# The gates' projection by Strassen's scheme (seven products of halves in place of eight), and the attentions' pools closed at their end

## The chip, the cores and the metric

The kernel runs on one core of one Trainium2 chip. The metric is device microseconds (us) of one execution; three runs of the kernel before stand below. All figures are of the core's five engines: PE (TensorE, matmuls), DVE (VectorE), ACT (ScalarE), POOL (GpSimd) and SP (SyncE, here only the queue that issues loads). PEld is the weight load of PE, which overlaps its matmuls. Each engine carries out its own list of instructions strictly in the order in which it stands; an instruction whose inputs are missing holds up everything behind it on the same engine.

## What is computed

One layer of four parallel mixers on 512 positions of width 1024. Cut to what matters here:

```
h    = rms_norm(x, norm_g)
proj = h @ w_in                       # 1024 -> 11208 columns, split into a_u, ..., d_z and gates
y_a, y_b, y_c, y_d = four mixers (spatial gating, sparse attention, convolution, attention), each * silu(z)
branch_d = einsum('nbsw,nwd->bsnd', ys, w_branch)       # 4 branches, 512 -> 1024
g        = sigmoid(gates.reshape(b, s, 4, 1024))        # gates: the last 4096 columns of proj
merged   = sum_n g_n * branch_d_n
out      = rms_norm(x + merged @ w_out, final_g)
```

The gates are 4096 of the 11208 projected columns, the largest single product of the kernel.

## The kernel before

Every product is in float32r: each operand is split into a high and a low part (`split`: ACT copies to the rounded high part, then another engine subtracts to get the low part), and a product is three matmuls per slice of 128 inputs: high by high, high by low, low by high. The normalized input stands transposed in SBUF as `hh` (high) and `hl` (low), 8 slices of 128 inputs by 512 positions.

`proj_fm` (L114 to L125) makes one tile of 128 projected columns by 512 positions: 24 matmuls, each of 128 weight columns and 512 positions. Its weights come as `raw` (1 MB, 256 columns, two buffers, loaded on SP's queue) and go through `unit` (L109): one split of 128x1024 elements for each 128 columns, by ACT (L80) and, for the low part, by POOL during the attentions and by DVE afterwards (L81, `weights_by`).

After the two attentions (FOX, then DSA) and the convolution come four times a pair of stages, for the branches C, A, D, B in this order:

- `gated` (L718): four tiles of 128 columns of z are projected, passed through a sigmoid (ACT, L726), multiplied by the mixer's output (POOL, L727), by z (DVE, L729), and split into `yh`, `yl`.
- `merge` (L736): eight tiles of 128 gate columns are projected (two to a load of `raw`, so four loads or *pairs*), each passed through a sigmoid (ACT, L771). `product` (L739) multiplies the branch's y by `w_branch` (12 matmuls of 512 positions, `pb`, L744 to L747), DVE multiplies by the gate (L750, L752) and POOL adds to `acc` (L753). A product is issued one projection later than its gate. Weights of the branch come as `rawb`, from the same two buffers as `raw`.

At the end `units_tm` and the `ps_o` products multiply by `w_out`; the last tile's `ps_o` is made in two halves of 256 columns.

A scheduler orders the instructions of each engine within what their data and buffers allow; the loads, splits, matmuls and evictions of one projection then stand beside the matmuls of the one before. There is no order written out by hand around the change. Buffers of SBUF belong to pools: `sb` holds tiles of the tag "qk" and "pt" for the attentions, `wpool` the weights' high and low parts (tags "wh", "wl", four buffers each), `const` small constants and the scores `sc1` to `sc3`.

Of the kernel before, what the change touches and what calls it, by code (L numbers as in the profile page):

```python
# [11 lines left out]
ALU = mybir.AluOpType  # L12
# [21 lines left out]
def hybrid_kernel(ctx: ExitStack, tc, x, norm_g, w_in, gm_ln_g, gm_ln_b, gm_w_s, gm_b_s,  # L34
# [19 lines left out]
    def qk_tile(name, dtype=F32R, shape=(P, 4, 512)):  # L54
        return sb.tile(list(shape), dtype, tag="qk", name=name, bufs=2)

    def pt_tile(name, dtype=F32R, shape=(P, 4, 512)):
        return sb.tile(list(shape), dtype, tag="pt", name=name, bufs=2)

# [46 lines left out]
    def wtiles(shape):  # L106
        return tuple(wpool.tile(shape, F32R, tag="w" + s, name="w" + s, bufs=4) for s in "hl")

# [79 lines left out]
    def load_dv(i):  # L188
# [17 lines left out]
    nc.vector.memset(negh, -0.5)  # L206
    causal = const.tile([P, P], F32, name="causal")
# [3 lines left out]
    up = const.tile([P, S], F32R, name="up")  # L211
    upf = tmp("upf")
# [120 lines left out]
    for u in range(2):  # L333
# [38 lines left out]
        else:  # L372
# [11 lines left out]
            nc.vector.tensor_tensor(cn, rb_, cn, op=ALU.mult)  # L384
            cth = const.tile([P, S], F32R, name="cth")
            ctl = const.tile([P, S], F32R, name="ctl")
            split(cth, ctl, cn, kvg)
# [326 lines left out]

    weights_by["eng"] = nc.vector


    def gated(col, o):  # L718
        y = pair("y")
        for cp in range(2):  # L720
            rz = load_w(col + cp * 256)
            for s in range(2):
                ct = 2 * cp + s
                ps = proj_fm(unit(rz, s))
                sg = tmp("sg")
# [9 lines left out]
    def merge(n, y, first, last):  # L735
        yh, yl = y  # L736
        pend = []

        def product():  # L739
            sg, bh, bl, s, dt = pend.pop()  # L740
            pb = psum("pb")
            cs_ = slice(s * P, (s + 1) * P)
            for k in range(NH):
                nc.tensor.matmul(pb, bh[:, k, cs_], yh[:, k, :], start=(k == 0), stop=False)  # L744
                nc.tensor.matmul(pb, bh[:, k, cs_], yl[:, k, :], start=False, stop=False)  # L745
            for k in range(NH):
                nc.tensor.matmul(pb, bl[:, k, cs_], yh[:, k, :], start=False, stop=(k == NH - 1))  # L747
            acc = accs[dt // 4][:, dt % 4, :]
# [9 lines left out]
        for dq in range(2):  # L758
# [5 lines left out]
            for dp in range(2):  # L764
                rg = load_w(GATES + n * D + (2 * dq + dp) * 256)
                bh, bl = wtiles([P, NH, 256])
                split(bh, bl, rb[:, :, dp * 256:(dp + 1) * 256])
                for s in range(2):
                    ps = proj_fm(unit(rg, s))
                    sg = tmp("sg")  # L770
                    nc.scalar.activation(sg, ps, AF.Sigmoid)  # L771
                    if pend:
                        product()
                    pend.append((sg, bh, bl, s, 4 * dq + 2 * dp + s))
        product()
# [94 lines left out]
```

## Time and profile before

| what | us |
|---|---|
| three runs | 711.07, 710.71, 709.07 |
| their median | 710.71 |
| the profiled execution | 711.89 |
| its span in the trace | 710.2 |
| PE busy | 693.9 (98% of the span) |
| DVE, ACT, POOL busy | 364.5, 275.1, 169.9 |

The profiled execution is 1.18 us longer than the median of the runs and 1.7 us longer than its own span in the trace. The attentions and the convolution end at about 311.7 us of the span; the four pairs of `gated` and `merge` follow until about 660 us, then `w_out`.

The duration of a matmul in the trace includes its passage through the array, and consecutive ones overlap: what one costs in a row of them is the distance between two starts, not its duration. In a timeline each line is one instruction or a run of equal ones (x8): start, duration, engine, line of the kernel, operation, output<-inputs, shape.

### The profile page before, as it was taken

How to read it: one execution, taken by the hardware profiler on the slowest of the kernel's cores; microseconds unless marked ns; L12 is line 12 of the kernel's file. 1: busy time of each engine (PE TensorE's matmuls, PEld its weight loads, DVE VectorE, ACT ScalarE, POOL GpSimd, SP SyncE). 2: the span in 40 equal slices, each digit the busy share in tenths (PEclk: the TensorE clock that was granted, in tenths of full speed). 3: DMA queues.
4: the chain of work that ended last, by engine and by line, in shares of the span. 5: the costliest groups of instructions: out<-in, count | busy, mean ns of one | idle time of the engine just before them, and what ended most of it. 6: DMA issues, size and time to landing. Idle time of an engine off the chain costs nothing.

```text
span 710.2 us, 8000 instructions
## 1 busy us (share of the span) xinstructions
PE 693.9 (98%) x3139; PEld 566.4 (80%) x3139; DVE 364.5 (51%) x638; ACT 275.1 (39%) x439; POOL 169.9 (24%) x110
## 2 busy tenths in 40 slices
PE   7999999988999999999999999999999999999996
PEld 4878767766888888888888888888888888888885
DVE  5825699999953664634233343323522334343454
ACT  4616354354444556433322242223322223333233
POOL 1000487341333323203000021222211132111101
PEclk9999999999999999999999999999999999999999
DMA  6715031312112111242322331322313313133233
GB/s 237 219 64 153 4 118 59 112 59 69 60 60 90 60 60 60 61 147 73 105 83 96 118 114 65 119 77 102 120 60 118 117 61 119 60 118 119 62 117 119
DMA packets 56817, 68.05 MB, mean 96 GB/s; under 512 B 3582, under 2 KB 45067, under 8 KB 56780
## 3 DMA queue, kind: packets, MB, share of 16 engines
q1 hardware_dynamic: 55900, 65.46, 28.3%
q0 software_dynamic: 304, 1.05, 0.4%
q10 hardware_dynamic: 576, 1.05, 0.4%
q8 instruction: 24, 0.39, 0.2%
q14 instruction: 13, 0.11, 0.0%
HBM read 64.80 MB, written 2.10 MB: 94 GB/s over the span
## 4 chain that ended last, share of the span: by engine, by line
PE 85%; DVE 11%; DMA 2%; issue 1%; ACT 0%; SPq 0%; POOLq 0%; POOL 0%; DVEq 0%
PE ps_fm L119 18%; PE ps_fm L120 18%; PE ps_fm L124 18%; PE pb L744 4%; PE pb L745 4%; PE pb L747 4%; DVE sc L474 3%; DVE m L473 2%; PE ps_o L144 2%; PE ps_o L146 2%; PE ps_o L145 2%; DVE sc L466 1%; PE pt_ps L533 1%; PE ps_dv L144 1%; DVE l L511 1%
## 5 line engine op out<-in xcount | busy, mean ns | idle before, releaser
L119 PE MATMUL ps_fm<-hh,wh 128*128 128x512 f32 (+1 forms) x640 | 251.3, 393 | 0.0
L120 PE MATMUL ps_fm<-hl,wh 128*128 128x512 f32 (+1 forms) x640 | 250.0, 391 | 0.0
L124 PE MATMUL ps_fm<-hh,wl 128*128 128x512 f32 (+1 forms) x640 | 162.5, 391 | 0.0
L119 PEld LDWEIGHTS ps_fm<-hh,wh 128*128 128x128 f32 (+1 forms) x640 | 120.1, 188 | 26.0 <-issue 0.9
L120 PEld LDWEIGHTS ps_fm<-hl,wh 128*128 128x128 f32 (+1 forms) x640 | 120.0, 187 | 24.9 <-issue 0.2
L124 PEld LDWEIGHTS ps_fm<-hh,wl 128*128 128x128 f32 (+1 forms) x640 | 119.0, 187 | 25.0 <-issue 0.2
L80 ACT ACTIVATE wh<-raw 128x1024 fp32r<-128x1024 f32 x78 | 82.3, 1056 | 114.1 <-PE ps_fm L120 85.0
L81 DVE TENSOR_TENSOR wl<-raw,wh 128x1024 fp32r<-128x1024 f32 x50 | 61.0, 1222 | 78.4 <-PE ps_fm L124 67.1
L81 POOL TENSOR_TENSOR wl<-raw,wh 128x1024 fp32r<-128x1024 f32 x28 | 69.1, 2474 | 111.9 <-PE ps_fm L124 49.2
L753 POOL TENSOR_TENSOR acc<-acc,sg 128x512 f32<-128x512 f32 x24 | 41.8, 1742 | 155.9 <-DVE sg L752 155.9
L744 PE MATMUL pb<-yh,wh 128*128 128x512 f32 x128 | 49.8, 389 | 0.0
L745 PE MATMUL pb<-yl,wh 128*128 128x512 f32 x128 | 49.8, 389 | 0.0
L81 DVE TENSOR_TENSOR wl<-rawb,wh 128x1024 fp32r<-128x1024 f32 x16 | 19.6, 1225 | 51.3 <-PE ps_fm L124 36.8
L80 ACT ACTIVATE wh<-rawb 128x1024 fp32r<-128x1024 f32 x16 | 16.9, 1057 | 50.6 <-PE ps_fm L120 50.6
L752 DVE TENSOR_TENSOR sg<-pb,sg 128x512 f32<-128x512 f32 x24 | 16.6, 692 | 36.3 <-PE pb L747 36.3
L747 PE MATMUL pb<-yh,wl 128*128 128x512 f32 x128 | 34.2, 389 | 0.0
L519 ACT ACTIVATE l<-l,nm 128x128 f32<-128x128 f32 (+3 forms) x32 | 17.9, 560 | 28.5 <-DVE nm L517 28.5
L771 ACT ACTIVATE sg<-ps_fm 128x512 f32<-128x512 f32 x32 | 19.2, 600 | 24.4 <-PE ps_fm L124 24.4
L747 PEld LDWEIGHTS pb<-yh,wl 128*128 128x128 f32 x128 | 24.0, 188 | 5.0
L744 PEld LDWEIGHTS pb<-yh,wh 128*128 128x128 f32 x128 | 24.0, 188 | 5.0
L745 PEld LDWEIGHTS pb<-yl,wh 128*128 128x128 f32 x128 | 24.0, 188 | 5.0
L145 PE MATMUL ps_o<-wl,mh 128*128 128x512 f32 (+1 forms) x72 | 26.2, 366 | 0.0
(242 smaller groups left out, 913.9 us busy)
## 6 DMA issues: line engine op xcount, KB each, us to landing
raw<-in_w_in_dram SPq DMA_DIRECT2D x39, 1024.0 KB, 4.9
rawb<-in_w_branch_dram SPq DMA_DIRECT2D x8, 1024.0 KB, 4.9
rawt<-in_w_out_dram SPq DMA_DIRECT2D x4, 1024.0 KB, 4.9
xt<-in_x_dram SPq DMA_DIRECT2D x4, 512.0 KB, 8.3
rawt<-in_w_in_dram SPq DMA_DIRECT2D x4, 512.0 KB, 8.4
rawt<-in_w_in_dram SPq DMA_DIRECT2D x2, 1024.0 KB, 5.7
xr<-in_x_dram SPq DMA_DIRECT2D x2, 1024.0 KB, 4.9
out_dram<-o SPq DMA_DIRECT2D x4, 256.0 KB, 2.1
```

Of the source, the lines that this page charges most:

```text
L80: nc.scalar.activation(hi, src, AF.Copy)
L81: eng.tensor_tensor(lo, src, hi.bitcast(F32), op=ALU.subtract)
L119: nc.tensor.matmul(ps[:m], wh[:, k, :], hh[:, k, :], start=(k == 0), stop=False)
L120: nc.tensor.matmul(ps[:m], wh[:, k, :], hl[:, k, :], start=False, stop=False)
L124: nc.tensor.matmul(ps[:m], wl[:, k, :], hh[:, k, :], start=False, stop=(k == NK - 1))
L144: nc.tensor.matmul(ps, ah, wh, start=(k == 0), stop=False)
L145: nc.tensor.matmul(ps, ah, wl, start=False, stop=False)
L474: nc.vector.match_replace(out=scs[i], in_to_replace=m8, in_values=scs[i], imm_value=TAKEN)
L744: nc.tensor.matmul(pb, bh[:, k, cs_], yh[:, k, :], start=(k == 0), stop=False)
L745: nc.tensor.matmul(pb, bh[:, k, cs_], yl[:, k, :], start=False, stop=False)
L747: nc.tensor.matmul(pb, bl[:, k, cs_], yh[:, k, :], start=False, stop=(k == NH - 1))
L753: nc.gpsimd.tensor_tensor(acc, acc, sg, op=ALU.add)
```

## The change

`early` is a pool of its own for what only the attentions and the stages before need (the tags "qk", "pt", "wh", "wl", and `causal`, `up`, `cth`, `ctl`, `sc1` to `sc3`). It is closed after the convolution, and a pool `late` is laid over its place. In it stand weights split by halves (`quarter`: 4 slices of inputs, 128x512 elements, tags "qh", "ql", eight buffers each), the sums `T1` to `T4` and the sums `s1` to `s4`.

A pair of gate tiles (256 columns) is one product of a 2x2 matrix of blocks (two halves of the columns by two halves of the inputs) and a 2x2 matrix of blocks of h (two halves of the inputs by two halves of the positions). Before, that is 8 block products, as 48 matmuls of 512 positions. `gate_pair` forms seven (in Winograd's form): each is 12 matmuls of 256 positions (`half_product`), 84 in all. Their sums are made partly in PSUM (`pa` and `pc` go on accumulating after a partial sum was copied out) and partly by ACT and DVE. Sums of blocks of h (`T1` to `T4`) are made once, after the pool is closed; sums of blocks of the weights (`s1` to `s4`) are made by POOL for each pair. `gated` uses the quarters too (`proj_q`, 24 matmuls of 512 positions as before). A product of the branch is now issued between the block products, of the pair before, so two instead of one are left at the end of a merge. `w_out` is split in eight parts of 128x512 instead of four of 128x1024, and the load of `final_g` waits for the place of `T1`.

```diff
+    early_scope = ExitStack()
+    early = early_scope.enter_context(tc.tile_pool(name="early", bufs=1))
...
     def qk_tile(name, dtype=F32R, shape=(P, 4, 512)):
-        return sb.tile(list(shape), dtype, tag="qk", name=name, bufs=2)
+        return early.tile(list(shape), dtype, tag="qk", name=name, bufs=2)
...
-    weights_by["eng"] = nc.vector
-
+    early_scope.close()
+    late = ctx.enter_context(tc.tile_pool(name="late", bufs=1, reuse_waits="tile"))
+
+    def quarter(src, shape=(P, 4, P)):
+        wh, wl = (late.tile(list(shape), F32R, tag="q" + x, name="q" + x, bufs=8) for x in "hl")
+        split(wh, wl, src)
+        return wh, wl
+
+    def half_product(ps, w, bh, bl, start, stop=True):
+        wh, wl = w
+        for k in range(4):
+            nc.tensor.matmul(ps, wh[:, k, :], bh[:, k, :], start=start and k == 0, stop=False,
+                             skip_group_check=True)
+            nc.tensor.matmul(ps, wh[:, k, :], bl[:, k, :], start=False, stop=False,
+                             skip_group_check=True)
+        for k in range(4):
+            nc.tensor.matmul(ps, wl[:, k, :], bh[:, k, :], start=False, stop=stop and k == 3,
+                             skip_group_check=True)
...
+    T1, T2, T3, T4 = (tsum("t%d" % i) for i in range(1, 5))
+    for kp in range(2):
+        r11, r12, r21, r22 = (sb.tile([P, 2, H], F32, tag="tmp", name="r", bufs=9) for _ in range(4))
+        for r, kh, th in ((r11, 0, 0), (r12, 0, 1), (r22, 1, 1), (r21, 1, 0)):
+            ks, ts_ = slice(4 * kh + 2 * kp, 4 * kh + 2 * kp + 2), slice(th * H, th * H + H)
+            nc.gpsimd.tensor_tensor(r, hh[:, ks, ts_].bitcast(F32), hl[:, ks, ts_].bitcast(F32),
+                                    op=ALU.add)
+        ks = slice(2 * kp, 2 * kp + 2)
+        for (th_, tl_), r, ra, rb_ in ((T1, r11, r12, r11), (T3, r12, r22, r12), (T2, r22, r22, r11),
+                                    (T4, r21, r21, r22)):
+            nc.vector.tensor_tensor(r, ra, rb_, op=ALU.subtract)
+            split(th_[:, ks, :], tl_[:, ks, :], r)
...
+    def gate_pair(raw, between):
+        a11, a12 = raw[:, 0:4, 0:P], raw[:, 4:8, 0:P]
+        a21, a22 = raw[:, 0:4, P:2 * P], raw[:, 4:8, P:2 * P]
+        s1, s2, s3, s4 = (late.tile([P, 4, P], F32, tag="s", name="s", bufs=4) for _ in range(4))
+        nc.gpsimd.tensor_tensor(s1, a21, a22, op=ALU.add)
+        nc.gpsimd.tensor_tensor(s2, s1, a11, op=ALU.subtract)
+        nc.gpsimd.tensor_tensor(s4, a12, s2, op=ALU.subtract)
+        nc.gpsimd.tensor_tensor(s3, a11, a21, op=ALU.subtract)
...
+        pa = bank("pa")
+        half_product(pa, quarter(a11), *fm(0, 0), True)
+        nc.scalar.activation(xu[:, lo], pa, AF.Copy)
+        pc = bank("pc")
+        half_product(pc, quarter(s1), *T1, True)
+        nc.scalar.activation(q, pc, AF.Copy)
+        between(0)
+        half_product(pa, quarter(s2), *T2, False)
+        nc.scalar.activation(xu[:, up_], pa, AF.Copy)
+        pb_ = bank("pb_")
+        half_product(pb_, quarter(a12), *fm(1, 0), True)
+        nc.vector.tensor_tensor(g1[:, lo], pb_, xu[:, lo], op=ALU.add)
+        half_product(pc, quarter(s4), *fm(1, 1), False)
+        nc.vector.tensor_tensor(g1[:, up_], pc, xu[:, up_], op=ALU.add)
+        nc.scalar.activation(g1, g1, AF.Sigmoid)
+        half_product(pa, quarter(s3), *T3, False)
+        nc.vector.tensor_tensor(g2[:, up_], pa, q, op=ALU.add)
+        nc.scalar.activation(g2[:, up_], g2[:, up_], AF.Sigmoid)
+        between(1)
+        half_product(pa, quarter(a22), *T4, False)
+        nc.scalar.activation(g2[:, lo], pa, AF.Sigmoid)
+        return g1, g2
...
-                rg = load_w(GATES + n * D + (2 * dq + dp) * 256)
-                bh, bl = wtiles([P, NH, 256])
-                split(bh, bl, rb[:, :, dp * 256:(dp + 1) * 256])
+                gs = gate_pair(load_w(GATES + n * D + (2 * dq + dp) * 256), product)
                 for s in range(2):
-                    ps = proj_fm(unit(rg, s))
...
+                    c0 = dp * 256 + s * P
+                    pend.append((gs[s], quarter(rb[:, :, c0:c0 + P]), 4 * dq + 2 * dp + s))
+        product()
         product()
```

Up to the end of the convolution all engines keep the order that they had, but for the splits of the weights of the first `gated`, which leave the convolution's rows, and the load of `final_g`. Two places after it show what moves.

The list of ACT at the end of the attentions, before; `pth` are the attention's transposed probabilities, `od` its output, `wh<-raw` and `wh<-rawb` weights' high parts (the first two of them for the last convolution tile and for a tile of z):

```order
L80 ACTIVATE pth<-pt_ps 128x3x128
L80 ACTIVATE wh<-raw 128x1024
L80 ACTIVATE pth<-pt_ps 128x4x128
L80 ACTIVATE wh<-raw 128x1024
L545 ACTIVATE od<-po 128x512
L80 ACTIVATE wh<-raw 128x1024
L80 ACTIVATE wh<-rawb 128x1024
L726 ACT_TABLE_LOAD
```

The same place now, with the buffers' numbers; `t1` to `t4` are the high parts of the sums of h, `qh` the quarters of the first z weights:

```order
L83 ACTIVATE pth_2647<-pt_ps_2731 128x4x128
L548 ACTIVATE od_1982<-po_2755 128x512
L83 ACTIVATE t1_2818<-r_2822 128x512
L83 ACTIVATE t3_2820<-r_2823 128x512
L83 ACTIVATE t2_2819<-r_2825 128x512
L83 ACTIVATE t4_2821<-r_2824 128x512
L83 ACTIVATE t1_2818<-r_2842 128x512
L83 ACTIVATE t3_2820<-r_2843 128x512
L83 ACTIVATE t2_2819<-r_2845 128x512
L83 ACTIVATE t4_2821<-r_2844 128x512
L83 ACTIVATE qh_2866<-raw_2864 128x512
```

The weights of z no longer stand among the attention's last rows: the first of them stands behind all eight splits of the sums of h.

The list of POOL from the convolution's last step (`cv`) through the first `gated` into the first `merge`, before:

```order
L696 TENSOR_SCALAR cv<-cc,prm 128x512 x2
L801 DMA fgB<-in_final_g_dram 128x1024
L727 TENSOR_TENSOR sg<-sg,oc 128x512 x4
L727 TENSOR_TENSOR sg<-sg,oa 128x512 x4
L753 TENSOR_TENSOR acc<-acc,sg 128x512 x8
```

The same place now; `r` are sums of the high and low parts of blocks of h, `s` the sums of blocks of the gates' weights:

```order
L699 TENSOR_SCALAR cv<-cc,prm 128x512 x2
L762 TENSOR_TENSOR r<-hh,hl 128x512 x8
L822 TENSOR_TENSOR sg<-sg,oc 128x512
L779 TENSOR_TENSOR s<-raw 128x512
L780 TENSOR_TENSOR s<-s,raw 128x512
L822 TENSOR_TENSOR sg<-sg,oc 128x512
L781 TENSOR_TENSOR s<-raw,s 128x512
L782 TENSOR_TENSOR s<-raw 128x512
L822 TENSOR_TENSOR sg<-sg,oc 128x512 x2
L779 TENSOR_TENSOR s<-raw 128x512
```

POOL's list had four multiplications in the first `gated` and none in the first `merge`; eight sums of h now stand ahead of the first multiplication, and the four sums of each pair's weights stand between and behind them.

## Rows read from the trace of the kernel before

**Rows 1.** The page: busy time, share and count of PE; its granted clock, forty slices.

```profile
PE 693.9 (98%) x3139; PEld 566.4 (80%) x3139; DVE 364.5 (51%) x638; ACT 275.1 (39%) x439; POOL 169.9 (24%) x110
PEclk9999999999999999999999999999999999999999
```

**Rows 2.** Windows: stretch, its length, busy time of each engine, clock, DMA share, GB/s.

```profile
344.00:667.00 323.00, 323.00 (x1427) 267.54 (x1426) 116.10 (x123) 98.55 (x122) 62.34 (x36) 1.00 0.30 98
```

**Rows 3.** Timeline of PE in a merge: starts of two products and two projections.

```profile
480.37 0.39 PE L744 MATMUL pb<-yh,wh 128*128 128x512 f32 x1
...
483.09 0.39 PE L744 MATMUL pb<-yh,wh 128*128 128x512 f32 x1
...
485.81 0.39 PE L119 MATMUL ps_fm<-hh,wh 128*128 128x512 f32 x1
...
491.25 0.39 PE L119 MATMUL ps_fm<-hh,wh 128*128 128x512 f32 x1
```

**Rows 4.** Timeline of PE: first and last of the 48 matmuls of 256 columns.

```profile
698.01 0.28 PE L144 MATMUL ps_o<-wh,mh 128*128 128x256 f32 x1
...
703.64 0.28 PE L146 MATMUL ps_o<-wh,ml 128*128 128x256 f32 x1
```

**Rows 5.** Groups by form: count, busy us, mean ns of one, idle before and its releasers.

```profile
L80 ACT ACTIVATE wh<-raw 128x1024 fp32r<-128x1024 f32 x78 | 82.3, 1056 | 114.1 <-PE ps_fm L120 85.0 <-PE pb L745 25.0 <-PE ps_va L146 2.6
L81 DVE TENSOR_TENSOR wl<-raw,wh 128x1024 fp32r<-128x1024 f32 x50 | 61.0, 1222 | 78.4 <-PE ps_fm L124 67.1 <-ACT wh L80 11.3
L771 ACT ACTIVATE sg<-ps_fm 128x512 f32<-128x512 f32 x32 | 19.2, 600 | 24.4 <-PE ps_fm L124 24.4
L81 DVE TENSOR_TENSOR yl<-y,yh 128x512 fp32r<-128x512 f32 x16 | 11.1, 693 | 11.2 <-ACT yh L80 11.2
L80 ACT ACTIVATE yh<-y 128x512 fp32r<-128x512 f32 x16 | 10.1, 632 | 40.6 <-DVE y L729 40.6
```

**Rows 6.** Timeline of PE: end of the convolution's last projection, start of z's first.

```profile
309.92 1.98 PE L124 MATMUL ps_fm<-hh,wl 128*128 128x512 f32 x8
311.73 0.39 PE L119 MATMUL ps_fm<-hh,wh 128*128 128x512 f32 x1
```

**Rows 7.** Timeline of POOL from the convolution's last step to the first z.

```profile
299.46 1.60 POOL L696 TENSOR_SCALAR cv<-cc,prm 128x512 f32<-128x512 f32 x1 [6.36 <-DVE cc L693]
307.49 0.60 POOL L801 DMA_DIRECT2D fgB<-in_final_g_dram  x1 [6.43 <-PE po L90]
318.63 1.28 POOL L727 TENSOR_TENSOR sg<-sg,oc 128x512 f32<-128x512 f32 x1 [10.54 <-ACT sg L726]
```

**Rows 8.** Timeline of DVE over the same stretch.

```profile
298.67 0.69 DVE L693 TENSOR_TENSOR cc<-ps_fm,cc 128x512 f32<-128x512 f32 x1 [2.15 <-PE ps_fm L124]
299.28 1.21 DVE L81 TENSOR_TENSOR wl<-raw,wh 128x1024 fp32r<-128x1024 f32 x1
300.41 0.68 DVE L81 TENSOR_TENSOR ptl<-pt_ps,pth 128x512 fp32r<-128x512 f32 x1
301.09 1.54 DVE L699 SCALAR_TENSOR_TENSOR cv<-cc,prm,cv 128x511 f32<-128x511 f32 x2
```

**Rows 9.** DVE (first two) and POOL (next two) timelines at 97 to 112 us; POOL's additions (min/median/max).

```profile
99.07 1.60 DVE L466 SCALAR_TENSOR_TENSOR sc<-relu,prm,sc 128x384 f32<-128x384 f32 x1
110.41 1.70 DVE L81 TENSOR_TENSOR val<-vn,vah 128x512 fp32r<-128x512 f32 x1
97.56 2.69 POOL L81 TENSOR_TENSOR wl<-raw,wh 128x1024 fp32r<-128x1024 f32 x1
109.82 1.75 POOL L610 TENSOR_TENSOR vn<-vn,gmp 128x512 f32<-128x512 f32 x1
L753 POOL TENSOR_TENSOR acc<-acc,sg x24: 1283/1714/2205, 435.1 to 661.0; 128x512 f32<-128x512 f32 x24
```

**Rows 10.** The page: loads of weights, count, KB each, us from issue to landing.

```profile
raw<-in_w_in_dram SPq DMA_DIRECT2D x39, 1024.0 KB, 4.9
```

**Rows 11.** Windows of 1 us in and behind PE's longest gap (columns as in rows 2).

```profile
168.00:169.00 1.00, 0.31 (x1) 0.30 (x2) 1.00 (x3) 1.00 (x4) 1.00 (x1) 1.00 0.00 0
170.00:171.00 1.00, 1.00 (x6) 1.00 (x6) 1.00 (x4) 0.39 (x3) 0.07 (x1) 0.50 0.02 8
173.00:174.00 1.00, 1.00 (x6) 0.82 (x5) 1.00 (x4) 0.31 (x1) 0.00 (x0) 1.00 1.07 377
```

More of the change, by code (lines that the diff above doesn't have):

```diff
@@ L54, in qk_tile @@
     def qk_tile(name, dtype=F32R, shape=(P, 4, 512)):
[L55 removed]
+        return early.tile(list(shape), dtype, tag="qk", name=name, bufs=2)
     def pt_tile(name, dtype=F32R, shape=(P, 4, 512)):
[L58 removed]
+        return early.tile(list(shape), dtype, tag="pt", name=name, bufs=2)
     def pair(name):
@@ L106, in wtiles @@
     def wtiles(shape):
-        return tuple(wpool.tile(shape, F32R, tag="w" + s, name="w" + s, bufs=4) for s in "hl")
+        return tuple(early.tile(shape, F32R, tag="w" + s, name="w" + s, bufs=4) for s in "hl")
     def unit(raw, s):
@@ L206, in hybrid_kernel @@
     nc.vector.memset(negh, -0.5)
-    causal = const.tile([P, P], F32, name="causal")
+    causal = early.tile([P, P], F32, name="causal")
     nc.gpsimd.memset(causal, 0.0)
@@ L210, in hybrid_kernel @@
                             pattern=[[-1, P]], channel_multiplier=1)
-    up = const.tile([P, S], F32R, name="up")
+    up = early.tile([P, S], F32R, name="up")
     upf = tmp("upf")
@@ L384, in hybrid_kernel @@
             nc.vector.tensor_tensor(cn, rb_, cn, op=ALU.mult)
-            cth = const.tile([P, S], F32R, name="cth")
-            ctl = const.tile([P, S], F32R, name="ctl")
+            cth = early.tile([P, S], F32R, name="cth")
+            ctl = early.tile([P, S], F32R, name="ctl")
             split(cth, ctl, cn, kvg)
@@ L450, in scores_topk @@
             n = (i + 1) * P
-            sc = const.tile([P, n], F32, name="sc%d" % i)
+            sc = early.tile([P, n], F32, name="sc%d" % i)
             scs[i] = sc
@@ new lines, in proj_q, with tsum @@
+    def proj_q(raw, s):
+        cs_ = slice(s * P, (s + 1) * P)
+        w = [quarter(raw[:, 4 * i:4 * i + 4, cs_]) for i in range(2)]
+        ps = mm.tile([P, S], F32, tag="mm", name="ps_z")
+        for i in range(2):
+            half_product(ps, w[i], hh[:, 4 * i:4 * i + 4, :], hl[:, 4 * i:4 * i + 4, :], i == 0, i == 1)
+        return ps
+    H = S // 2
+    def tsum(name):
+        t = late.tile([P, 2, 4, H], F32R, tag="ts", name=name, bufs=4)
+        return t[:, 0], t[:, 1]
+    T1, T2, T3, T4 = (tsum("t%d" % i) for i in range(1, 5))
@@ new lines, in fm, with bank @@
+    def fm(k, t):
+        return hh[:, 4 * k:4 * k + 4, t * H:t * H + H], hl[:, 4 * k:4 * k + 4, t * H:t * H + H]
+    def gate_pair(raw, between):
[6 more added lines that the diff above has]
+        nc.gpsimd.tensor_tensor(s3, a11, a21, op=ALU.subtract)
+        g1, g2 = tmp("g1"), tmp("g2")
+        xu, q = tmp("xu"), tmp("q", cols=H)
+        lo, up_ = slice(0, H), slice(H, S)
+        def bank(name):
+            return mm.tile([P, S], F32, tag="mm", name=name)[:, lo]
+        pa = bank("pa")
[20 more added lines that the diff above has]
+        return g1, g2
@@ L723, in gated @@
                 ct = 2 * cp + s
-                ps = proj_fm(unit(rz, s))
+                ps = proj_q(rz, s)
                 sg = tmp("sg")
@@ L737, in merge, with product @@
         pend = []
-        def product():
-            sg, bh, bl, s, dt = pend.pop()
+        def product(_=None):
+            if not pend:
+                return
+            sg, (bh, bl), dt = pend.pop(0)
             pb = psum("pb")
-            cs_ = slice(s * P, (s + 1) * P)
             for k in range(NH):
-                nc.tensor.matmul(pb, bh[:, k, cs_], yh[:, k, :], start=(k == 0), stop=False)
-                nc.tensor.matmul(pb, bh[:, k, cs_], yl[:, k, :], start=False, stop=False)
+                nc.tensor.matmul(pb, bh[:, k, :], yh[:, k, :], start=(k == 0), stop=False)
+                nc.tensor.matmul(pb, bh[:, k, :], yl[:, k, :], start=False, stop=False)
             for k in range(NH):
-                nc.tensor.matmul(pb, bl[:, k, cs_], yh[:, k, :], start=False, stop=(k == NH - 1))
+                nc.tensor.matmul(pb, bl[:, k, :], yh[:, k, :], start=False, stop=(k == NH - 1))
             acc = accs[dt // 4][:, dt % 4, :]
@@ L788, in hybrid_kernel @@
         cs_ = slice(half * 512, (half + 1) * 512)
-        us = units_tm(w_out[0], cs_)
+        us = []
+        for kh in range(2):
+            raw = load_tm(w_out[0], kh, cs_)
+            us += [quarter(raw[:, j, :], (P, 512)) for j in range(4)]
         xr = raw_tile([P, NT, 512], "xr")
@@ L793, in contrib @@
         def contrib(ps, t, k, c):
-            wh, wl = us[k // 2]
+            wh, wl = us[k]
             mh, ml = mrg[k // 4]
             ts_ = slice(t * P, (t + 1) * P)
-            term_tm(ps[:, c], mh[:, k % 4, ts_], ml[:, k % 4, ts_], wh[:, k % 2, c], wl[:, k % 2, c], k)
+            term_tm(ps[:, c], mh[:, k % 4, ts_], ml[:, k % 4, ts_], wh[:, c], wl[:, c], k)
         if half == 0:
-            fgB = pt_tile("fgB", F32, (P, D))
+            fgB = late.tile([P, D], F32, tag="ts", name="fgB", bufs=4)
             nc.gpsimd.dma_start(fgB, bcast_rows(final_g, D))
```

5 lines of the change are left out of this document (removed).

## The prediction, made before the changed kernel ran

> **What bounds the kernel now.** I read the page's shares of busy time first. PE is busy 693.9 of 710.2 us, its granted clock stands at full in nearly every slice [rows 1], DVE comes to about half of that. The average could hide a stage, so the second view is the windows: from 344 to 667 us, which holds the merges, PE is busy 323.00 of 323.00 us at clock 1.00, while DVE needs 116, ACT 99 and POOL 62 [rows 2]. Nothing but less work for PE can shorten this stretch, and every microsecond that PE waits there, now or after the change, is added whole. The third view is the timeline of PE: the rate of a row of matmuls is the distance of starts. A projection's 24 matmuls of 512 positions run from 485.81 to 491.25, 0.2267 us each; a product's 12 take 2.72 [rows 3].
>
> **What the change takes off PE.** Per pair of gate tiles 48 matmuls of 512 positions become 84 of 256. The only long row of 256 columns stands at the tail: from the first to the last of 48 starts 5.63 us, over 47 distances 0.1198 each [rows 4]. Half of 0.2267 is 0.1133, so each half matmul carries 0.0064 us of its own. There are 4 merges of 4 pairs: 16 x 48 x 0.2267 = 174.1 us go, 16 x 84 x 0.1198 = 161.0 come, which is **-13.1**. By the count of columns alone it would be 174.1/8 = 21.8; the small extra takes 8.7 of it. The Trainium skill ("TensorE: Matmul & The Clock Gate", "Back-to-back issue gap") gives about 131 ns for a sustained matmul of 512 columns and 81 ns at 128; two of 256, an estimate between these, would then cost more than one of 512, and the change would be slower by tens of us. Both rows speak against that here, so it enters no term.
>
> **What it adds on other engines.** Per pair POOL makes four sums of 128x512 elements, in addition to two accumulations; one such operation takes 1.28 us alone [rows 7] and 1.28 to 2.2 in a merge [rows 9]. Why up to 2.2: DVE operations with two inputs in SBUF and POOL operations don't run side by side here. A DVE operation that begins at 99.07 ends at 100.67, just behind the end of POOL's split at 97.56 + 2.69 = 100.25; a second ends at 112.11, behind POOL's end at 109.82 + 1.75 = 111.57 [rows 9]. A waiting engine gets in at the other's end. The Trainium skill ("SBUF — State Buffer", "Who interferes with whom") says that such a pair shares one read port, taken by whichever issues first for its whole length; it speaks against this change, which puts sums on both engines at once. The two rows agree with it; by it the transition below costs 8.8, without it 2.8.
>
> Per pair this shared path then carries 6 x 1.28 = 7.7 us of POOL and nine DVE splits of half size (seven quarters of the gate, two of the branch). A DVE split of 1024 takes 1.22, one of 512 positions 0.69 [rows 5]; half of the former is 0.61, I take 0.65: 9 x 0.65 = 5.9. Together 13.6, against PE's 84 x 0.1198 + 24 x 0.2267 = 15.5 per pair. It fits, narrowly; a chain in it need not.
>
> **The transition.** Before, z's first weights are split on ACT and DVE well ahead; z's first projection follows the convolution's last one at 311.73 without a gap [rows 6]. Now eight sums on POOL, eight subtractions on DVE and eight splits of the T sums stand ahead of the first quarter of z, on both engines. No row shows them. The walk:
> - POOL is free for them after the last `cv`: 299.46 + 1.60 = 301.06 [rows 7], and DVE still has two steps of 1.54 together for the last `cv` [rows 8].
> - If the two engines exclude each other, one path holds 8 x 1.28 + 1.54 + 8 x 0.65 = 17.0 us, to 318.0. Then DVE has one output of the convolution, eight low halves of T and the first low quarter of z: 0.61 + 8 x 0.61 + 0.69 = 6.2, to **324.2**. (0.61 is also the distance of two starts on DVE, 298.67 to 299.28 [rows 8].)
> - ACT has T's last high half and the first high quarter at 0.63 each [rows 5], to 319.3. PE can run 16 matmuls with high quarters before it needs the first low one. Undisturbed that one would be due at 311.73 + 16 x 0.2267 = 315.4. Loss 324.2 - 315.4 = 8.8.
> - PE then has stood for about 7 us. After a gap of PE in the kernel before the granted clock was 0.50 from 170 to 171 and back at 1.00 by 173 [rows 11], so 2.4 GHz falls to 1.2 and returns in some 3 us. The 16 matmuls cover most of that while ql is awaited; 16 x 0.2267 = 3.6 is the most it can add, I take none.
>
> Bounds: without exclusion POOL ends at 301.06 + 10.24 = 311.3, DVE's last subtraction at 312.0, the low quarter at 318.2: loss 2.8. With exclusion and a slow clock 12.4. I take **+8.8**, as rows 9 show the exclusion twice.
>
> **The first merge.** The first load of gate weights for a later pair waits for a buffer that z's last quarters release. In the kernel before a load of 1 MB lands 4.9 us after its issue [rows 10]. With the low quarters 0.61 apart, z's last is cut at about 324.2 + 7 x 0.61 = 328.5 and that load lands at 333.4; the last z projection ends at 311.73 + 4 x 5.44 + 8.8 = 342.3. That is 9 us ahead, but the sums of the weights share POOL with the four multiplications of z, and ACT's copy `q` of the first partial sum stands behind a split that waits for the next load. Walking the queues through the first pair gives waits of PE of 1.4 us at the bank of the third block product, freed late by a DVE multiplication, and 2.3 at the one with `s4`: **+3.7**, from 1 (exclusion absent) to 6.
>
> **The later merges.** There the loads come earlier. The same walk leaves slack of about 0.5 us at two places per merge: `q` behind the split of the next load, and the copies of `pa` behind the sum `s2`. I take 0.3 for each merge, three of them: **+1.0**, from 0 to 8.
>
> **Edits at nothing.** The splits of `w_out` have half the size and twice the number on engines far from full [rows 2]; the last two products of a merge, where one stood, are followed by PE's own work. Fewer ACT evictions (0.60 each, 32 of them [rows 5]) are replaced by seven half-size ones per pair, on an engine busy 99 of 323 us. The load of `final_g`, POOL 0.60 [rows 7], moves behind the use of `T1`, and is needed only in the tail. If one of these shows, it is below 1 us each.
>
> **Sum.** 711.89 - 13.1 + 8.8 + 3.7 + 1.0 = 712.3 for the profiled execution, which is 1.18 above the median of the runs, so **711.1** as a median.
>
> **Rivals.**
> 1. *The gain arrives.* POOL and DVE do run side by side on these shapes, or the waiting engine gets in more cheaply: transition 2.8, first merge 2, later ones 0.5. 711.89 - 13.1 + 5.3 - 1.18 = **702.9**. For it: that POOL is busy only 62 of 323 us [rows 2], so that most of its work can find room. Against it: rows 9, and that the eight sums stand in one row with the eight subtractions.
> 2. *The pairs are bound by the chain, slower.* One buffer of raw weights serves all four pairs of a merge in turn while the other holds the branch's weights; next load (4.9 us [rows 10]), sums `s1`, `s2`, `s4` (3 x 1.28 at least, up to 3 x 2.2 [rows 9]), split, matmul is a chain within each pair of 15.5 us. If each of POOL's sums is stretched to the 1.71 that is the median of the accumulations [rows 9], six of them take 10.3 rather than 7.7; the 2.6 more eat the 0.5 of slack and PE loses 2.1 in each of the 12 later pairs at worst, or about 0.6 if the loads ahead absorb most. At 0.6 a pair: 711.1 + 12 x 0.6 - 1.0 = **717.3**. It decides from 0.2 us per pair on, which is slower by over 0.3%. For it: the narrow 13.6 against 15.5; against it: median 1.71 is with splits of double size, whose halves block less long.
> 3. *The matmuls of 256 don't keep 0.1198* with other halves of `hh` as the moving side: at 0.130 the 1344 matmuls give back 13.7 us and the change gains nothing: 711.1 + 13.7 = 724.8. Only the tail row [rows 4] speaks to it, and against it.
>
> **How the numbers follow.** Forecast (PE gains 13, waits take all of it back, to within 0.3%, which is about what a measurement of this kernel can tell from no change: 708.6 to 712.8): 0.35, its own range 707 to 714 before it passes into the rivals. Rival 1: 0.33. Rival 2: 0.28, rival 3: 0.04. Faster 0.33, same 0.35, slower 0.32. The range reaches from 702.5, which leaves a third of rival 1 out, to 719, which leaves out rival 3 and a fifth of rival 2: some 0.2 in all.
>
> **What would show it.** Right: a gap of PE of about 7 us behind the convolution's last projection, ended by ACT's first quarter, and then a wait for DVE's `ql`; POOL's eight sums and DVE's subtractions alternating from 301 to 318; starts of the half products 0.12 apart; waits of PE in the first merge at `pb_` and at the product with `s4`; later merges with PE busy throughout. Wrong: subtractions running beside POOL's sums, PE gaps in every pair, or starts 0.13 apart.

## The result: slower by 2.8%

| | before | after |
|---|---|---|
| median of the runs, us | 710.89 | 730.88 |
| lowest and highest | 709.07, 711.99 | 729.57, 731.95 |
| span of the profiled execution | 710.2 | 728.8 |
| z's first projection starts / `w_out` starts | 311.7 / 659.9 | 314.9 / 678.5 |

The ratio is 1.0283 (95% interval 1.0259 to 1.0307). The forecast was 711.1 with a range up to 719.0: the change is slower by 20 us, outside the range.

The page of the changed kernel first (columns as in [rows 1]):

```profile
PE 693.9 (95%) x3715; PEld 591.0 (81%) x3715; DVE 493.4 (68%) x822; ACT 330.4 (45%) x631; POOL 276.6 (38%) x182
PEclk9999999989999999999999999999999899999998
```

PE has 576 matmuls more, of half the size, and exactly the busy time that it had: what the change saves there was lost again, mostly on slower matmuls (table below). The span is longer by 18.6 us, all of it idle time. The window that answers to [rows 2], a little longer since the stage is:

```profile
344.00:678.00 334.00, 320.08 (x1979) 289.54 (x1978) 224.26 (x278) 149.64 (x294) 151.72 (x97) 0.97 0.30 99
```

Before, PE was busy for all of the stretch at clock 1.00; now 14 us are missing and the clock is 0.97. POOL went from 62 to 152 us, DVE from 116 to 224.

To see how the loss divides I took the starts of PE's rows from its timeline and compared their distances with 0.2267 us for 512 positions and 0.1198 for 256 [rows 3, 4]. The column on the clock holds the matmuls that started while the granted clock was 0.50; the last one holds mostly waits of 0.1 to 0.2 us and the part of each long wait that the end of the matmul ahead of it covers.

| stretch (us) | over those distances | idle, in waits over 0.3 | matmuls at clock 0.50 | the rest |
|---|---|---|---|---|
| 308.2 to 338.3, end of convolution and z | 6.6 | 4.7 | 1.6 | 0.3 |
| 338.3 to 411.1, first merge | 10.7 | 5.9 | 3.1 | 1.7 |
| 411.1 to 499.5, second z and merge | 4.7 | 3.4 | 0.0 | 1.3 |
| 499.5 to 590.6, third | 7.3 | 3.3 | 2.8 | 1.2 |
| 590.6 to 678.5, fourth | 4.2 | 2.2 | 1.6 | 0.4 |
| sum | 33.5 | 19.5 | 9.1 | 4.9 |

Less the 13.1 that the smaller products save this is 20.4. The spans differ by 18.6, since PE also ended the convolution some 1.7 us earlier in this execution; that point lies between 308 and 312.5 us in the runs.

The same wait stands in merges one to three, 2.73 or 2.74 us each: PE stands in front of the third pair's last block product, with the fourth pair begun. This is PE's timeline there in the first merge (start, duration, engine, line, operation; in brackets the idle time and what ended it):

```profile
387.45 0.40 PE L840 MATMUL pb<-yh,qh 128*128 128x512 f32 x1
390.57 0.58 PE L732 MATMUL pa<-t,qh 128*128 128x256 f32 x1 [2.73 <-DVE g L806]
390.95 0.41 PE L734 MATMUL pa<-t,qh 128*128 128x256 f32 x1
391.17 0.41 PE L732 MATMUL pa<-t,qh 128*128 128x256 f32 x1
```

PE has the last block product of the third pair before it, which goes on accumulating in `pa`; DVE must first have read `pa` into `g2` (L806). Behind the wait the starts lie 0.21 to 0.22 apart, not 0.12. DVE's timeline over the same stretch:

```profile
383.89 1.23 DVE L84 TENSOR_TENSOR ql<-raw,qh 128x512 fp32r<-128x512 f32 x1 [5.00 <-ACT qh L83]
385.04 0.41 DVE L803 TENSOR_TENSOR g<-pc,xu 128x256 f32<-128x256 f32 x1
385.37 1.44 DVE L84 TENSOR_TENSOR ql<-s,qh 128x512 fp32r<-128x512 f32 x1
386.74 0.68 DVE L846 TENSOR_TENSOR acc<-pb,g 128x512 f32<-128x512 f32 x1
387.34 1.18 DVE L84 TENSOR_TENSOR ql<-s,qh 128x512 fp32r<-128x512 f32 x1
388.44 1.75 DVE L84 TENSOR_TENSOR ql<-raw,qh 128x512 fp32r<-128x512 f32 x1
390.11 0.41 DVE L806 TENSOR_TENSOR g<-pa,q 128x256 f32<-128x256 f32 x1
```

And POOL's:

```profile
383.27 1.29 POOL L779 TENSOR_TENSOR s<-raw 128x512 f32<-128x512 f32 x1 [8.88 <-DMA raw<-in_w_in_dram]
384.65 1.62 POOL L780 TENSOR_TENSOR s<-s,raw 128x512 f32<-128x512 f32 x1
386.35 1.61 POOL L781 TENSOR_TENSOR s<-raw,s 128x512 f32<-128x512 f32 x1
387.93 1.71 POOL L782 TENSOR_TENSOR s<-raw 128x512 f32<-128x512 f32 x1
```

Read together: the load of the fourth pair lands at about 383.2, POOL and DVE have both stood idle for it, and both start within 0.7 us. The four sums run in a row; the four splits of the new pair beside them take 1.18 to 1.75 us where 0.65 was assumed, two-input operations whose ends follow POOL's ends (385.12 behind 384.56, 386.81 behind 386.27, 388.52 behind 387.96, 390.19 behind 389.64). The operation for which PE waits, 0.41 us long, is the seventh in that row. The operations with one input in PSUM (L803, L846) keep their 0.41 and 0.68.

In the fourth merge PE waits for the load itself: ACT splits it as soon as it has landed, and PE starts behind ACT (first ACT, then PE).

```profile
652.57 0.63 ACT L83 ACTIVATE qh<-raw 128x512 fp32r<-128x512 f32 x1 [4.64 <-DMA raw<-in_w_in_dram]
653.25 0.49 PE L732 MATMUL pa<-hh,qh 128*128 128x256 f32 x1 [2.17 <-ACT qh L83]
```

Merges two and three have the same kind of wait, 0.66 and 0.54 us, some 6.7 us ahead of the long one. Of the 8.8 us of waits in merges two to four, 3.4 are thus for the load and 5.5 for DVE's addition.

What follows the wait in the first merge is seen in windows of PE (columns as in [rows 2]):

```profile
388.00:390.00 2.00, 0.00 (x0) 0.00 (x0) 2.00 (x2) 0.63 (x1) 1.64 (x1) 1.00 0.00 0
390.00:392.00 2.00, 1.43 (x6) 1.43 (x7) 1.60 (x4) 1.45 (x4) 0.00 (x0) 0.64 0.00 0
392.00:394.00 2.00, 2.00 (x10) 1.90 (x9) 1.30 (x3) 1.56 (x4) 0.00 (x0) 0.51 0.00 0
394.00:396.00 2.00, 2.00 (x11) 1.68 (x11) 0.43 (x2) 0.63 (x1) 0.00 (x0) 1.00 0.93 292
```

PE was idle for 2.7 us; then the granted clock falls to 0.5, from 2.4 to 1.2 GHz, for some three us although PE is busy throughout, and returns. Such stretches make the clock's column of the table, 9.1 us in all. Not every wait has one. In the second merge the wait for DVE is as long and the clock stays at full speed:

```profile
480.53 0.39 PE L732 MATMUL pa<-t,qh 128*128 128x256 f32 x1 [2.73 <-DVE g L806]
```

```profile
479.00:481.00 2.00, 0.47 (x4) 0.47 (x5) 2.00 (x3) 0.49 (x2) 2.00 (x2) 1.00 0.00 0
481.00:483.00 2.00, 2.00 (x15) 1.83 (x14) 2.00 (x3) 2.00 (x6) 0.28 (x1) 1.00 0.00 0
483.00:485.00 2.00, 2.00 (x14) 1.80 (x13) 1.39 (x4) 0.94 (x3) 0.00 (x0) 1.00 0.38 97
```

Of the five waits of over 2 us in the merges four had a stretch at 0.50, of 3.4 us each and in the third merge of 6.8.

### The profile page after: what moved, and what is told of

The parts are those of the page before. It is cut to its first block, busy times and chain, and to the rows that moved or that the text cites. A ratio compares the mean times of both kernels' runs of the same rounds, so it can differ in the third digit from the quotient of the medians.

```text
span 728.8 us, 9819 instructions
## 1 busy us (share of the span) xinstructions
PE 693.9 (95%) x3715; PEld 591.0 (81%) x3715; DVE 493.4 (68%) x822; ACT 330.4 (45%) x631; POOL 276.6 (38%) x182
## 4 chain that ended last, share of the span: by engine, by line
PE 50%; DVE 24%; DMA 12%; issue 7%; POOL 4%; ACT 3%; SPq 0%; POOLq 0%; DVEq 0%; ACTq 0%
DMA raw<-in_w_in_dram 10%; DVE ql L84 8%; PE ps_fm L122 5%; PE ps_fm L127 5%; PE ps_fm L123 5%; DVE sc L477 3%; DVE m L476 3%; PE pb L843 2%; PE pb L841 2%; ACT qh L83 2%; PE pb L840 2%; PE pa L732 2%; PE ps_o L147 2%; PE ps_o L148 2%; PE ps_o L149 2%
## 5 line engine op out<-in xcount | busy, mean ns | idle before, releaser
L84 DVE TENSOR_TENSOR ql<-raw,qh 128x512 fp32r<-128x512 f32 x80 | 75.5, 951 | 80.0 <-ACT qh L83 65.0
L122 PE MATMUL ps_fm<-hh,wh 128*128 128x512 f32 (+1 forms) x256 | 102.9, 403 | 0.0
L123 PE MATMUL ps_fm<-hl,wh 128*128 128x512 f32 (+1 forms) x256 | 101.8, 398 | 0.0
L84 DVE TENSOR_TENSOR ql<-s,qh 128x512 fp32r<-128x512 f32 x64 | 73.4, 1161 | 4.3 <-ACT qh L83 3.9
L127 PE MATMUL ps_fm<-hh,wl 128*128 128x512 f32 (+1 forms) x256 | 68.0, 396 | 0.0
L779 POOL TENSOR_TENSOR s<-raw 128x512 f32<-128x512 f32 x16 | 20.6, 1289 | 106.6 <-DMA raw<-in_w_in_dram 106.6
L732 PE MATMUL pa<-t,qh 128*128 128x256 f32 x192 | 50.5, 293 | 8.2 <-DVE g L806 8.2
L122 PEld LDWEIGHTS ps_fm<-hh,wh 128*128 128x128 f32 (+1 forms) x256 | 48.6, 190 | 11.3 <-issue 1.2
L123 PEld LDWEIGHTS ps_fm<-hl,wh 128*128 128x128 f32 (+1 forms) x256 | 48.5, 190 | 10.2 <-issue 0.2
L127 PEld LDWEIGHTS ps_fm<-hh,wl 128*128 128x128 f32 (+1 forms) x256 | 47.1, 187 | 10.1 <-issue 0.2
L734 PE MATMUL pa<-t,qh 128*128 128x256 f32 x192 | 50.1, 291 | 0.0
L732 PEld LDWEIGHTS pa<-t,qh 128*128 128x128 f32 x192 | 38.2, 199 | 10.3 <-DVE g L806 9.1
L734 PEld LDWEIGHTS pa<-t,qh 128*128 128x128 f32 x192 | 38.4, 200 | 0.8
```

Of the source, the lines that this page charges most:

```text
L84: eng.tensor_tensor(lo, src, hi.bitcast(F32), op=ALU.subtract)
L122: nc.tensor.matmul(ps[:m], wh[:, k, :], hh[:, k, :], start=(k == 0), stop=False)
L123: nc.tensor.matmul(ps[:m], wh[:, k, :], hl[:, k, :], start=False, stop=False)
L127: nc.tensor.matmul(ps[:m], wl[:, k, :], hh[:, k, :], start=False, stop=(k == NK - 1))
L732: nc.tensor.matmul(ps, wh[:, k, :], bh[:, k, :], start=start and k == 0, stop=False, skip_group_check=True)
L734: nc.tensor.matmul(ps, wh[:, k, :], bl[:, k, :], start=False, stop=False, skip_group_check=True)
```

## The experiments

Two questions stood at the start: whether the waits of the merges come from the path that POOL and DVE share or from loads that land too late; and what the setup of `T1` to `T4` costs. All times are medians; ratios are to the kernel before, run on the same chip (710 to 711 us), with 95% intervals. Diffs are against the changed kernel.

**e1: POOL's sums only write.** The line of `s1`; `s2`, `s4` and `s3` likewise.

```diff
-        nc.gpsimd.tensor_tensor(s1, a21, a22, op=ALU.add)
+        nc.gpsimd.memset(s1, 0.01)
...
```

> POOL's four sums of each pair's gate weights are replaced by four POOL operations of the same size that only write (the sums are then a constant, so the gates are not the reference's); all else stays. Theory A (the shared path): the changed kernel loses 26 us in its merges because DVE's low splits of the weights run 1.2 to 1.8 us instead of 0.65 while POOL's sums read. Without those reads the splits take 0.65 to 0.7 and the waits of PE for DVE g of 2.7 us vanish: 708 to 714 us. Theory B (late loads): the gate weights land too late, since all four pairs of a merge use one buffer in turn; DVE's and POOL's work hardly matters, the waits stay near 2 us each: 726 to 731.

Measured: 706.26, ratio 0.9946 (0.9923 to 0.9969). The second, third and fourth stages of z and merge took 84.0 us each; their matmuls alone are 96 x 0.2267 + 336 x 0.1198 + 96 x 0.2267 = 83.8. As Theory A expected, but the edit took away two things, the reads and the chain from the load to the sums.

**e2: a buffer of its own for the branch's weights.** To make room, the fourth sum `s3` is also made later, behind the copy `q`, and the sums have three buffers instead of four.

```diff
-            rb = raw_tile([P, NH, 512], "rawb")
...
+                rb = late.tile([P, NH, 256], F32, tag="rb", name="rawb", bufs=1)
+                rg = load_w(GATES + n * D + cb)
+                nc.sync.dma_start(rb, w_branch[0, n, :, cb:cb + 256].rearrange("(k p) c -> p k c", p=P))
```

> The branch's weights get a buffer of their own (loads of 512 KB, 256 columns), so both 1 MB buffers serve the gates in turn; the fourth sum is made a little later to make room. Theory A: DVE's splits still take 1.2 to 1.8 us beside POOL's sums, and the order of the engines is much the same; some waits get shorter, 724 to 730 us. Theory B: the loads land 5 us and more ahead, the waits of PE in the later merges go, 710 to 716.

Measured: 706.78, ratio 0.9945 (0.9925 to 0.9964), better than either theory expected, again with stages of 84.0 us each. Groups by form over the second to fourth stage (count, busy us, mean ns, idle time before), the changed kernel first:

```profile
L84 DVE TENSOR_TENSOR ql<-raw,qh 128x512 fp32r<-128x512 f32 x53 | 52.3, 986 | 57.6 <-ACT qh L83 51.6 <-issue 4.9 <-PE pb__5354 L734 1.1
L84 DVE TENSOR_TENSOR ql<-s,qh 128x512 fp32r<-128x512 f32 x48 | 57.2, 1207 | 2.9 <-ACT qh L83 2.5
L779 POOL TENSOR_TENSOR s<-raw 128x512 f32<-128x512 f32 x12 | 15.5, 1290 | 79.1 <-DMA raw<-in_w_in_dram 79.1
```

and e2:

```profile
L84 DVE TENSOR_TENSOR ql<-raw,qh 128x512 fp32r<-128x512 f32 x54 | 52.8, 977 | 12.2 <-ACT qh L83 8.5 <-PE ps_z L737 3.4
L84 DVE TENSOR_TENSOR ql<-s,qh 128x512 fp32r<-128x512 f32 x48 | 41.3, 861 | 22.1 <-PE ps_z L737 9.6 <-ACT qh L83 7.4 <-PE pa L737 4.6
L779 POOL TENSOR_TENSOR s<-raw 128x512 f32<-128x512 f32 x11 | 15.2, 1385 | 11.7 <-issue 3.9 <-DMA raw<-in_w_in_dram 3.7 <-DVE ql L84 3.4
```

POOL waited 79 us for loads in the changed kernel and 3.7 here; DVE's splits are still long, 0.86 to 0.98 us in the mean (0.99 to 1.21 before), and PE waits for none of them in these stages. So neither theory holds alone. The edit also broke up POOL's row: the four sums of a pair no longer follow each other (they start at 448.5, 453.2, 455.0 and 461.8 us for one pair of the second stage), so this run takes away two things, too.

**e3: the sums of h behind the first z.** The block that makes `T1` to `T4` is written behind `yc = gated(C_Z, oc)`.

> The sums T1 to T4 of h are written behind the first stage of z instead of ahead of it. Both theories: the gap of 4.7 us before z's first projection and the slow clock behind it (1.7 us) go; if the sums then delay the first pair by as much, the time stays. Theory 'the setup costs 4.8 us' expects 725 to 727; a rival, that the sums only move their price into the first merge, 730 to 733.

Measured: 737.93, ratio 1.0391 (1.0371 to 1.0411): worse than both. The gap ahead of z is gone, but from z's start to the end of the first merge it takes 106.6 us against 96.2, with waits of up to 4.0 us for the splits of the sums, then between PE's single matmuls. The price only moved, and grew.

**e4: the pools and quarters alone.** `gate_pair` makes two plain projections; no sums.

> The pools are closed and the weights split by quarters as in the change, but the gates are projected by eight products (24 matmuls of 512 positions per tile) and no sums are made. If closing the pools and the quarters cost nothing by themselves, 709 to 713 us; if the moved splits ahead of z cost, 714 to 718.

Measured: 710.82, ratio 1.0003 (0.9987 to 1.0020). Closing the pools and splitting by quarters cost nothing; PE has no wait from 300 to 670 us.

**e5: as much POOL time, hardly a read.** Two `memset` of the sum, then one column of it formed from the operands.

> Two things fell in e1 at once: POOL no longer reads beside DVE, and its operations no longer wait for the load and for each other. Here each of the four sums is two operations that only write (0.53 us each in e1) and one that reads one column in 128 of the same operands, so POOL waits for the load and for its own chain as in the changed kernel, about 1.2 us a link, but hardly reads (the gates are not the reference's). Theory A (the shared path is what makes the chain too long): DVE's low splits take 0.65 to 0.75 us, the waits in the merges go, 705 to 712 us. Rival (POOL's chain from the load to the sums is itself too long, whatever DVE does): the waits of 2.7 us for DVE g stay, 722 to 731.

Measured: 705.94, ratio 0.9921 (0.9897 to 0.9944). Inconclusive: the writes depend on nothing, POOL's list had them ahead of the load, and behind it stood four operations of 0.21. The chain had fallen with the reads, as in e1.

**e6: the sums on DVE.** `nc.gpsimd` becomes `nc.vector` in the four lines.

> The four sums of each pair stand on DVE instead of POOL, one word in each of four lines; the loads keep their two buffers. Theory A: no POOL operation reads beside a split but the additions into acc, DVE does 4 x 0.69 = 2.8 us more a pair and comes to some 11 of 15.5; most waits go, 706 to 714 us. Rival (DVE becomes the bound, the sums queue in it behind the splits of the pair before): 718 to 730.

Measured: 709.46, ratio 0.9977 (0.9957 to 0.9998). The later stages take 84.0 to 84.1. In the first merge the wait of 2.2 for ACT's `q` stays.

**e7: e2, and two tiles of z ahead of the sums of h.** In `gated`; `mid` is the block that makes `T1` to `T4`.

```diff
+            pz = [proj_q(rz, s) for s in range(2)]
+            if mid is not None and cp == 0:
+                mid()
...
```

> e2's buffer for the branch's weights, and the first two tiles of z are projected ahead of the sums T of h, the other two behind; the high quarters of the first two stand on ACT ahead of T's splits. Of the 706.8 of e2 the gap of 4.85 us ahead of z and the 1.7 of the slow clock go, a wait of about 1.2 for the first low quarter comes: 700 to 703. If the sums then come late for the first pair as in e3: 706 to 714.

Measured: 703.48, ratio 0.9893 (0.9862 to 0.9924), just above the 700 to 703. The gap of 4.7 became a wait of 2.95 for `ql`, which DVE still gives only behind its eight subtractions, and 2.9 us lost on slow matmuls behind it, at clock 0.50 from 316 to 323 us (the 0.96 in the next run's expectation is too small); the first merge has no wait left.

**e8: e7, with the sums of the high and low parts of h on DVE too.**

> e7, and the eight sums of the high and low parts of h (the first step of T1 to T4) stand on DVE instead of POOL. In e7 PE still waited 2.95 us for the first low quarter and ran 0.96 longer at the slow clock, since DVE's eight subtractions alternated with POOL's sums, 15.2 us for both. Sixteen operations of 0.65 to 0.69 on DVE alone take 11, of which five stand ahead of the last step of the attention. If the shared path is what holds ql back, both losses go: 699 to 701 us. Rival (DVE's sums delay the attention's last product by as much as they save): 702 to 706.

Measured: 700.61, ratio 0.9865 (0.9838 to 0.9891): most of the gain arrives, 9.9 of the 13.1 us. Its window of the merges:

```profile
344.00:650.00 306.00, 306.00 (x1950) 278.97 (x1949) 200.69 (x276) 152.86 (x288) 133.99 (x94) 1.00 0.32 102
```

One wait is left behind 300 us, 1.5 us for DVE's `y` in the first merge.

**e9: e2 and e6 at once.**

> e2 and e6 at once: a buffer of its own for the branch's weights, and the four sums of each pair on DVE. Each alone gave 706.8 and 709.5. If the later merges lose only through the product of two causes (loads just in time, and splits made long by POOL's reads), there is nothing left to gain in them: 705 to 708. If the two are separate costs, the gains add: 690 or so (730.9 less 24 less 21).

Measured: 705.53, ratio 0.9937 (0.9913 to 0.9962). The two remedies don't add: each removes the same waits.

**e10 and e11: the chain without the reads, the reads without the chain.** In e10 the column is formed first and two `memset` write over it, so they have to wait; in e11 the four sums read `hh` and `hl`. The lines of `s1`, first e10, then e11:

```diff
+        nc.gpsimd.tensor_tensor(s1[:, :, 0:1], a21[:, :, 0:1], a22[:, :, 0:1], op=ALU.add)
+        nc.gpsimd.memset(s1, 0.01)
+        nc.gpsimd.memset(s1, 0.01)
...
+        nc.gpsimd.tensor_tensor(s1, hh[:, 0:4, 0:P].bitcast(F32), hl[:, 0:4, 0:P].bitcast(F32), op=ALU.add)
```

> In e5 POOL's writing operations ran ahead of the load, so its chain fell together with its reads. Here each sum is first one that reads one column in 128 of the sum's operands, then two operations of full size that write over it: each link waits for the load and the link before, and takes 0.21 + 2 x 0.53 = 1.27 us, but POOL hardly reads (the gates are not the reference's). Theory A1 (the splits that POOL's reads make long are what turns the just-in-time loads into waits): DVE's splits at 0.65 to 0.8, at most 0.7 us of wait a merge, 705 to 712. Theory A2 (POOL's chain behind a late load is enough): waits of 2 us and more in each merge, 718 to 730.

Measured for e10: 707.95, ratio 0.9950 (0.9936 to 0.9963). The fourth pair of the first merge, POOL and then DVE:

```profile
380.72 0.21 POOL L779 TENSOR_TENSOR s<-raw 128x4 f32<-128x4 f32 x1 [8.72 <-DMA raw<-in_w_in_dram]
380.99 0.53 POOL L780 MEMSET s<- 128x512 f32 x1
381.57 0.52 POOL L781 MEMSET s<- 128x512 f32 x1
382.17 0.21 POOL L782 TENSOR_TENSOR s<-s,raw 128x4 f32<-128x4 f32 x1
```

```profile
381.33 0.69 DVE L84 TENSOR_TENSOR ql<-raw,qh 128x512 fp32r<-128x512 f32 x1 [5.45 <-ACT qh L83]
381.94 0.42 DVE L811 TENSOR_TENSOR g<-pc,xu 128x256 f32<-128x256 f32 x1
382.79 0.69 DVE L84 TENSOR_TENSOR ql<-s,qh 128x512 fp32r<-128x512 f32 x1 [0.43 <-ACT qh L83]
383.40 0.68 DVE L854 TENSOR_TENSOR acc<-pb,g 128x512 f32<-128x512 f32 x1
384.25 0.69 DVE L84 TENSOR_TENSOR ql<-s,qh 128x512 fp32r<-128x512 f32 x1 [0.17 <-ACT qh L83]
384.86 0.69 DVE L84 TENSOR_TENSOR ql<-raw,qh 128x512 fp32r<-128x512 f32 x1
385.46 0.42 DVE L814 TENSOR_TENSOR g<-pa,q 128x256 f32<-128x256 f32 x1
```

Both engines idle for the load as before (8.7 and 5.5 us), the sums follow each other at 1.45, but the splits keep their 0.69 and L814, the former L806, starts 4.1 us behind the first split instead of 6.2. The stages two to four take 84.0 again. So POOL's chain behind a load for which it idles costs nothing where the splits are short. Against PE's own progress the load is not quite as late as it was: it lands 1.7 to 2.1 us ahead of PE's first matmul of the fourth pair, and 0.8 in the changed kernel, where PE waits for it in three merges. In e6, with no sum on POOL, it lands only 0.8 to 1.1 us ahead of that matmul in stages two to four, and PE doesn't wait.

> The converse: POOL's four operations per pair read the same number of elements as the sums, but from hh and hl, so nothing waits for the load and for each other (the gates are not the reference's). POOL holds the shared path as long as before. A1: the splits stay long (1.0 us and more) and the time with them, 718 to 730. A2: no chain behind the load, 705 to 712.

Measured for e11: 713.82, ratio 1.0044 (1.0025 to 1.0062), between the two theories. Its splits are long in the same stages, as A1 says:

```profile
L84 DVE TENSOR_TENSOR ql<-s,qh 128x512 fp32r<-128x512 f32 x48 | 50.0, 1058 | 1.5 <-ACT qh L83 1.4
L84 DVE TENSOR_TENSOR ql<-rawb,qh 128x512 fp32r<-128x512 f32 x24 | 26.0, 1095 | 6.8 <-ACT qh L83 6.8
```

yet stages two to four take 84.0, 84.0 and 85.0. What it loses is elsewhere: 6.5 us instead of 4.7 ahead of z, and 3.1 in the first merge, where the sums of the first pair now run right behind those of h (POOL goes on without a break from 300.2 to 320.1). So the long splits alone don't cost either, where POOL's reads are not in one row behind the load.

The waits of the later merges stood where three things met: a load that lands just in time, POOL's four sums in a row behind it, and the shared path that makes the splits of the same pair beside them 1.2 to 1.8 us long. Without POOL's reads (e10, e6) or without the row behind the load (e11) the stages take 84 to 85 us, with an early load and the row broken up (e2) 84. The three are not quite separate: no run moves the load alone, and in e10 and e11 it lands earlier against PE as well (1.9 to 2.6 us ahead of the fourth pair in e11, but for the last merge). How much each costs by itself is not shown.

## Why the prediction was wrong, step by step

- **PE's own gain, -13.1: right in size.** Undisturbed stages fell from 4 x 24 x 0.2267 + 192 x 0.2267 + 96 x 0.2267 = 87.0 to the 84.0 of e2, which is 3.0 per merge and 12 in all. The distance of 0.1198 held with blocks of h and with sums; rival 3 falls.
- **The transition, +8.8: right in kind, too large.** The eight sums and the subtractions alternate as walked; the row of POOL:

```profile
298.37 13.18 POOL L762 TENSOR_TENSOR r<-hh,hl 128x512 f32<-128x512 f32 x8
```

and of DVE:

```profile
301.83 3.48 DVE L767 TENSOR_TENSOR r<-r 128x512 f32<-128x512 f32 x2
305.23 0.68 DVE L710 TENSOR_TENSOR oc<-ps_fm,cv 128x512 f32<-128x512 f32 x1
305.83 7.79 DVE L767 TENSOR_TENSOR r<-r 128x512 f32<-128x512 f32 x6
313.53 0.68 DVE L710 TENSOR_TENSOR oc<-ps_fm,cv 128x512 f32<-128x512 f32 x1
314.13 4.89 DVE L84 TENSOR_TENSOR t<-r,t 128x512 fp32r<-128x512 f32 x8
```

  From the first sum to the last subtraction it is 15.2 us, where 17.0 was walked, from 298.4 and not 301.1. PE stood 4.7 us, not 7, and then lost 1.9, 1.6 of it at the lower clock, where the prediction took none: 6.6. No wait for `ql` followed, because the slow matmuls covered it: the first low quarter was there at about 319.6, and PE was through the 16 matmuls only at 320.2. The bounds 2.8 and 12.4 held.
- **The first merge, +3.7: two of three places.** The waits of 1.4 at the third block product and 2.3 at the one with `s4` came as 0.99 and 2.20. The wait of 2.73 for DVE's addition and the 3.1 at the lower clock were not in the walk; the stretch cost 10.7.
- **The later merges, +1.0 with an upper bound of 8: the step that failed.** They cost 16, of which 8.8 are waits and 4.4 matmuls at the lower clock. Its premise that the loads come earlier there held for the first pair of each merge, whose load landed 15 us ahead of PE, and not for the fourth, where it was 0.8 with PE waiting. The walk priced every split at 0.65 us, and put the shared path at 13.6 of 15.5 us per pair. With e10's 0.69 a split that sum is 13.9, so the mean was not wrong by much, but it is a mean: POOL's reads lie in one row of 6.4 us behind each load, and there the path is full and the splits take 1.2 to 1.8. The place was wrong too: not `q` and not `s2`, but DVE's addition into `g2` of the pair before, seventh in DVE's list behind splits of the next pair, and in the fourth merge the load itself.
- **The clock, "I take none": the second step that failed.** [rows 11] showed that a gap of under 2 us is followed by some three us at half speed. That was weighed only for the transition. Four of the five waits of over 2 us in the merges had such a tail; the tails came to 9.1 us with the transition's 1.6.
- **The rivals.** Rival 2 named the right cause, the one buffer, the sums behind the load, and POOL's stretch, and priced it at 0.6 us a pair; with the clock it was 16 over the 12 later pairs, 1.3 each. That was below the 2.1 that the same paragraph allowed "at worst" and then set aside with no row to say why. Rival 1 is what the kernel does once the load comes early and the transition is ordered (e8: 700.6).

Why merge four waits for the load and not for DVE can be read from PE's timeline: the load lands 15.9 us behind the one before it, as in merges two and three (16.2 and 16.0), but PE's list has only 11.6 us of work between the first products of the third and the fourth pair there, against 13.2. What stays open is why the wait of 2.73 us in merge two left the clock at full speed, and why the stretch behind the equal one in merge three was twice as long as that in merge one; no run took these apart.

## What to carry to other kernels

A change that takes work off a full engine and gives it to others must be costed in its bursts: where a load lands just in time, all that waits for it starts at once, and two engines that share a path meet there, whatever the mean says. Let the load land earlier, or take the bursts off the shared path. Moving the read that PE waits for ahead of the next unit's work in DVE's list suggests itself as well, but no run tried it. Here 4 KB per partition for a buffer of its own, two tiles of z ahead of the setup, and the setup's sums on one engine turned 730.9 into 700.6 us, against 710.5 before.

Price each wait of PE with a possible tail at the lower clock, not with its idle time alone: here a tail of 3.4 us cost about 1.5 us, and four of five waits of over 2 us in the merges had one.

## What the runs showed of the hardware that was not expected

- A POOL operation that only writes 128x512 elements (0.53 us) left DVE's two-input splits at 0.69 where it ran beside them (e10); one that reads as much made them 1.2 to 1.8. The Trainium skill ("SBUF — State Buffer", "Who interferes with whom") says that a DVE instruction with two SBUF inputs contends with a POOL instruction that reads SBUF, and not with one that only writes it; these rows agree.
- An idle time of PE of 2.7 us inside a stage that is otherwise full was followed by a granted clock of 0.50 for 3.4 us in one merge and for 6.8 in another, and by none in a third.
- Matmuls of 256 positions kept 0.12 us from start to start over stages of 84 us, 53% of one of 512, with new weights at each.
